# Two heads at once on the array's halves in attention and in the recurrence's chunk products, and modulation matmuls tied in fours

## The chip, the cores and the metric

The kernel runs on one core of a Trainium2 chip. The metric is the device time of one execution in microseconds (us). TensorE (PE in the profile, its weight loads PEld), VectorE (DVE), ScalarE (ACT) and GpSimd (POOL) each work through their own queue of instructions in order and wait for each other by semaphores; SyncE (SP) issues the transfers from memory. Matmul results land in PSUM, from where VectorE and ScalarE take them.

## The reference

Two decoder layers over 256 tokens of width 2048. In each, a vector `c` gives shifts, scales and gates (the modulation), one input projection feeds two groups of 16 heads of 64, and an output projection and a squared-ReLU MLP of width 8192 follow. Group A is RWKV-7 (a recurrence with a matrix state for each head), group B sparse attention with compressed, selected and window branches. At 256 tokens all four blocks of 64 tokens are selected and the window covers everything, so both of the latter are causal attention, each with keys and values of its own.

```
mod = silu(c) @ w_ada[i] + b_ada[i]            # six vectors of 2048: shift, scale, gate, twice
u = (x * (1 + sc_m) + sh_m) @ w_in[i]
# group A, per head:  sa = S @ -kk;  S = S * w + sa (kk a)^T + v k^T;  o = S @ r
# group B, per head:
p_cmp = softmax(where(cmask, q @ kc.T * scale, NEG)) * cmask      # 15 compressed keys
o = g0 * p_cmp @ vc + g1 * softmax(mask(q @ ks.T * scale)) @ vs + g2 * softmax(mask(q @ kw.T * scale)) @ vw
x = layer_norm(ALPHA * x + (1 + gt_m) * (concat(o_A, o_B) @ w_out[i]))
x = layer_norm(ALPHA * x + (1 + gt_f) * (relu(h @ w1)**2 @ w2))
```

## The kernel before

Activations are kept transposed, 128 features on the partitions and the 256 tokens along the row. The projections (`block`, L243, and `kouter`, L256) split each fp32 weight into a high part `wh` and a low part `wl` (`unit`, L218: one DMA of 512 KB, a cast on ScalarE, a subtraction on VectorE) and do three fp32r products for each pair of operands (`mm3`, L235). `block` makes one output tile of 128 rows from 48 matmuls; `kouter` makes eight at once, going through the inputs one by one. All other matmuls are plain fp32, and each of them stands in the trace as two records. The program is written in order of computation; a planner then puts every engine's instructions into a fixed order, by priority (by default the place in the program) and by when it expects operands and buffers to be ready. `tc.high_priority` raises the priority of what is traced inside it, and `tc.issue_after(ins)` makes what is traced inside it come after `ins` on the same engine. Tiles are taken from named groups of buffers: `st(tag, ...)` in SBUF, with the counts of `BUFS` (L175; one where no count stands), and `mx(th, ...)` in PSUM, one bank for `"m"` and `"n"`, two for `"a"` and `"c"`.

The modulation of layer 0 is made on TensorE by `ada_pe` (L357): for a group of 512 outputs, four steps, each of four matmuls. A matmul takes 128 rows of the weight (`wap`, 512 columns, in memory order from the `wad` tensors) as the moving operand and the vector, repeated over 32 columns, as the weights, and writes one quarter of the 128 partitions of `gv` (L369). The first eight groups run in the opening stage (`first`, `start`), whose TensorE order is the program's own. The other twelve (`mid_ada`, L689) are drawn step by step by `spread` and `extra` beside the projections of layer 0: the first seven groups with two DMAs of 512 KB a step (tag `wf`), the last five with four DMAs of 256 KB a step (tag `UR`, eight buffers). Layer 1's modulation and the rest of layer 0's are made on VectorE (`ada`, L334).

The recurrence works in chunks of 64 tokens. `rwkv_a` (L483) prepares a pair of heads (one on partitions 0 to 63, one on 64 to 127); for each head it builds the operand `ur` on VectorE, makes four chunk products `mt` of 64 by 128 by 128 (L530), masks and copies them out, and transposes (`bkt`, L541). There are four pairs in each half and two halves in each layer. `rwkv_b` inverts the chunk's triangular matrices, `rwkv_c` goes through the four chunks, `rwkv_out` normalises.

Attention (`attend`, L823) goes through eight pairs of heads `j`; `q` holds a pair's queries on both partition halves. It makes the compressed scores `cs` and their softmax, transposes them (`ct`), and opens the pair's output `o` (L851). Then for each of two branches `br` and each head `h` in turn: scores `sc` of 128 and 256 columns on the head's half of the rows (L856, L857), masked maxima on VectorE (L861, L862), exponentials with sums on ScalarE (L863, L864), reciprocal, gate and scaling (L865 to L868), three transposes into `pt` (L871), a copy to `pts` (L873), and two products into the head's half of the columns of `o` (L875, L876). The next pair's query projection, and in layer 1 the output projection's `kouter`, can run between.

## Time and profile before

| | us |
|---|---|
| time, median of 3 runs | 2917.93 |
| the runs | 2905.41, 2917.93, 2918.88 |
| the profiled execution, its own time | 2923.44 |
| its span, from the first to the last instruction | 2921.7 |
| PE busy in it | 2804.9 |
| DVE busy | 2103.1 |
| ACT busy | 1507.3 |

Durations below come from the profiled execution. "Busy" counts an engine from an instruction's start to its end; consecutive matmuls overlap in time, so a record's own duration is longer than the distance to the next start. The granted clock of TensorE is given as a share of full speed. An entry such as `gv<-wap,cT 128*32 128x512 f32 x8` reads: written tile, read tiles, the part of the array in use (rows by columns), the moving operand, and how many records follow each other.

### The profile page before, as it was taken

What the parts mean: (1) busy time and instruction counts of PE and PEld (TensorE: products, weight loads), DVE (VectorE), ACT (ScalarE), POOL (GpSimd) and SP (SyncE); (2) the same over time, 40 slices, a digit from 0 to 9 for tenths busy, and PEclk for the clock granted to TensorE, in tenths of its full rate; (3) what the DMA queues carried; (4) which work ended last, traced back from release to release, by engine and by line L of the source; (5) the groups of instructions that cost most, each with busy time, mean ns of one, the idle gap of its engine ahead of it and who ended that gap; (6) DMA issues with size and microseconds to landing.
All of it is one profiled execution on the core that took longest, in us unless ns stands there. A gap on an engine that the chain in (4) does not pass through costs nothing. (4 is left out here: it accounts for less than half of the span.)

```text
span 2921.7 us, 59534 instructions
## 1 busy us (share of the span) xinstructions
PE 2804.9 (96%) x22794; PEld 2502.9 (86%) x22794; DVE 2103.1 (72%) x4774; ACT 1507.3 (52%) x3221; POOL 68.6 (2%) x205
## 2 busy tenths in 40 slices
PE   7989999999999999999999999999999999999997
PEld 4677677745998999999999988887799999999997
DVE  3677768635787777888889787785788656666567
ACT  3344345534474454554645553455657555464555
POOL 0000010000000000000000000100000000000000
PEclk9999999999999999999999998998999999999998
DMA  9986655355658888888887634342275767777663
GB/s 319 315 261 213 238 193 158 103 172 194 221 171 309 308 307 305 319 312 316 320 317 229 191 115 165 107 128 63 80 253 174 243 207 238 234 223 223 194 191 129
DMA packets 206782, 639.64 MB, mean 219 GB/s; under 512 B 23392, under 2 KB 42848, under 8 KB 206496
## 3 DMA queue, kind: packets, MB, share of 16 engines
q1 hardware_dynamic: 206496, 635.83, 65.6%
q8 instruction: 179, 2.93, 0.4%
q14 instruction: 107, 0.88, 0.1%
HBM read 629.45 MB, written 6.29 MB: 218 GB/s over the span
## 5 line engine op out<-in xcount | busy, mean ns | idle before, releaser
L226 ACT CAST wh<-wf 128x512 fp32r<-128x512 f32 x1536 | 944.7, 620 | 916.3 <-PE acc L206 570.5
L227 DVE TENSOR_TENSOR wl<-wf,wh 128x512 fp32r<-128x512 f32 x1536 | 1032.2, 688 | 339.2 <-ACT wh L226 328.8
L206 PE MATMUL acc<-hhi,wl 128*128 128x256 f32 x3456 | 979.5, 284 | 22.0 <-DVE wl L227 21.7
L206 PE MATMUL acc<-hhi,wh 128*128 128x256 f32 x3456 | 982.1, 284 | 15.8 <-ACT wh L226 9.3
L206 PE MATMUL acc<-hlo,wh 128*128 128x256 f32 x3456 | 971.8, 282 | 0.0
L206 PE MATMUL acc<-hi,wl 128*128 128x256 f32 x2560 | 719.9, 281 | 19.5 <-DVE wl L227 19.0
L206 PE MATMUL acc<-lo,wh 128*128 128x256 f32 x2560 | 715.3, 280 | 2.0 <-DVE lo L215 2.0
L206 PE MATMUL acc<-hi,wh 128*128 128x256 f32 x2560 | 714.5, 279 | 1.0 <-DVE res L1030 0.7
L206 PEld LDWEIGHTS acc<-hhi,wh 128*128 128x128 f32 x3456 | 655.3, 190 | 69.8 <-issue 34.6
L206 PEld LDWEIGHTS acc<-hhi,wl 128*128 128x128 f32 x3456 | 655.2, 190 | 48.1 <-DVE wl L227 32.0
L206 PEld LDWEIGHTS acc<-hlo,wh 128*128 128x128 f32 x3456 | 654.1, 189 | 12.8 <-issue 9.2
L206 PEld LDWEIGHTS acc<-hi,wl 128*128 128x128 f32 x2560 | 483.7, 189 | 30.4 <-DVE wl L227 25.9
L206 PEld LDWEIGHTS acc<-lo,wh 128*128 128x128 f32 x2560 | 483.5, 189 | 5.3 <-DVE lo L215 2.6
L206 PEld LDWEIGHTS acc<-hi,wh 128*128 128x128 f32 x2560 | 483.6, 189 | 4.5 <-issue 1.8
L341 DVE CUSTOM_DVE_ANT_0 wa<-wa,cond,modh 128x1024 f32<-128x1024 f32 x112 | 143.6, 1282 | 58.6 <-DMA wa<-in_wada 58.0
L341 DVE CUSTOM_DVE_ANT_0 wa<-wa,cond,vec 128x1024 f32<-128x1024 f32 x112 | 143.6, 1282 | 46.8 <-DMA wa<-in_wada 46.5
L206 PE MATMUL gv<-wap,cT 128*32 128x512 f32 x640 | 149.0, 617 | 8.5 <-DMA wap<-in_wad 7.8
L288 DVE TENSOR_TENSOR sum<-sum,acc 128x512 f32<-128x512 f32 x70 | 48.0, 686 | 47.4 <-PE acc L206 47.4
L1070 DVE TENSOR_TENSOR lo<-relu,hi 128x256 fp32r<-128x256 f32 x128 | 53.9, 424 | 34.9 <-ACT relu L1069 34.8
L206 PE MATMUL sc<-Kd,q 64*128 64x128 f32 (+1 forms) x256 | 64.6, 366 | 0.0
L206 PE MATMUL ot<-pts,Vt 128*64 128x256 f32 (+1 forms) x256 | 57.7, 344 | 0.9 <-DVE pts L873 0.9
L206 PEld LDWEIGHTS gv<-wap,cT 128*32 128x32 f32 x640 | 21.3, 108 | 40.3 <-issue 12.3
(294 smaller groups left out, 2504.0 us busy)
## 6 DMA issues: line engine op xcount, KB each, us to landing
wf<-in_w SPq DMA_DIRECT2D x512, 512.0 KB, 4.8
wa<-in_wada SPq DMA_DIRECT2D x224, 512.0 KB, 5.3
wf<-in_win SPq DMA_DIRECT2D x192, 512.0 KB, 4.1
wap<-in_wad SPq DMA_DIRECT2D x208, 256.0 KB, 4.1
wf<-in_wout SPq DMA_DIRECT2D x64, 512.0 KB, 4.5
wap<-in_wad SPq DMA_DIRECT2D x56, 512.0 KB, 4.6
cw<-in_cw SPq DMA_DIRECT2D x16, 512.0 KB, 3.8
xin<-in_xT SPq DMA_DIRECT2D x16, 128.0 KB, 5.8
```

What stands on the lines that cost most here:

```text
L206: return PE.matmul(o, l, r, start=start, stop=stop, skip_group_check=True)
L226: A.copy(wh, wf[:, s])
L227: V.tensor_sub(wl, wf[:, s], wh.bitcast(FT))
L288: V.tensor_add(s, s, bank)
L341: V.tensor_tensor_reduce(wa, wa, cb, 0.5, init, OP.mult, OP.add, dst)
L1070: gate[0] = V.tensor_sub(lo, t, hi.bitcast(FT)).ins
```

## The change

Three places are rewritten. In `ada_pe` the last of a step's four matmuls is traced first, and the other three are traced with a high priority and an edge that keeps them behind it on TensorE. In `rwkv_a` the operands of both heads are built first, into two banks, and the chunk products alternate between the heads, chunk by chunk; evictions follow, head by head. In `attend` both heads of a pair are handled together within a branch: their scores go to two banks of group `"a"`, the first one carries a dependency on the maximum last traced, and the other three follow it; reciprocals and gates are made for both at once; transposes and copies are grouped by key block instead of by head (`PT0` 512 columns on ScalarE, `PT1` 256 columns on VectorE, one buffer each), and the products into `o` run for both heads one behind the other. The compressed scores move from bank `"n"` to bank `"m"`, the output `o` from the two banks `"a"` to the one bank `"n"`, and `P` holds both heads in one tile for each branch.

```diff
--- before.py
+++ after.py
@@ -173,7 +173,7 @@
         psp = ctx.enter_context(tc.tile_pool(name="psp", bufs=1, space=PSUM))
         drp = ctx.enter_context(tc.tile_pool(name="drp", bufs=1, space=bass.MemoryType.DRAM))
         BUFS = {"S": 52, "OG": 4, "wf": 5, "wh": 4, "wl": 4, "UR": 8, "TM": 8, "BK": 8, "SV": 2, "QB": 2, "ZV": 2, "Us": 2, "rk": 4, "sh": 2,
-                "loa": 1, "loc": 1, "sm": 2, "PT": 2, "pc": 2, "tya": 6, "tyc": 6, "tyn": 8,}
+                "loa": 1, "loc": 1, "sm": 1, "pc": 2, "tya": 6, "tyc": 6, "tyn": 8,}
 
         def st(tag, shape, dt=FT, name=None):
             if dbg is not None:
@@ -364,9 +364,14 @@
                     part = src[u0 + u * n // 2].rearrange("p (a b) -> p a b", a=2)
                     SY.dma_start(w, part if n == 2 else part[:, u % 2:u % 2 + 1])
                     ws += [w[:, k] for k in range(n)]
-                for c in range(4):
+                def part_mm(c):
                     kt = 4 * q + c
-                    mm(gv[c * 32:c * 32 + 32], cT[:, kt:kt + 1].to_broadcast([128, 32]), ws[c], q == 0, q == 3)
+                    return mm(gv[c * 32:c * 32 + 32], cT[:, kt:kt + 1].to_broadcast([128, 32]), ws[c], q == 0, q == 3).ins
+
+
+                with tc.issue_after(part_mm(3)), tc.high_priority(3000000):
+                    for c in range(3):
+                        part_mm(c)
                 yield
             w = 512 // len(gs)
             for i, g in enumerate(gs):
@@ -518,16 +523,19 @@
 
                 V.scalar_tensor_tensor(sq, r, vc(l, "rk", pi), kp, op0=OP.mult, op1=OP.mult)
 
-                for h in range(2):
-                    me, ot = slice(h * 64, h * 64 + 64), slice(64 - h * 64, 128 - h * 64)
+                halves = [(slice(h * 64, h * 64 + 64), slice(64 - h * 64, 128 - h * 64)) for h in range(2)]
+                mts = [mx("a", [128, 4, 128], "mt") for h in range(2)]
+                for h, (me, ot) in enumerate(halves):
                     ur, tm = st("UR", [128, 4, 128]), st("TM", [128, 4, 128])
                     H["UR"][p][h], H["TM"][p][h] = ur, tm
                     G.memset(tm, 0.0)
                     V.tensor_mul(ur[me, :, 0:64], c4(kkn)[me], P[me, :, 0:64])
                     V.tensor_mul(ur[me, :, 64:128], c4(r)[me], P[me, :, 1:65])
-                    mt = mx("a", [128, 4, 128], "mt")
-                    for c in range(4):
-                        mm(mt[:, c], bk[me, c, h:h + 2].rearrange("p a b -> p (a b)"), ur[me, c])
+                for c in range(4):
+                    for h, (me, ot) in enumerate(halves):
+                        mm(mts[h][:, c], bk[me, c, h:h + 2].rearrange("p a b -> p (a b)"), H["UR"][p][h][me, c])
+                for h, (me, ot) in enumerate(halves):
+                    ur, tm, mt = H["UR"][p][h], H["TM"][p][h], mts[h]
                     rm = cs("rmask")
                     V.tensor_mul(ur[ot], mt[ot], rm[ot, None, :].to_broadcast([64, 4, 128]))
                     V.tensor_mul(tm[me, :, 64:128], mt[me, :, 64:128], rm[me, None, 64:128].to_broadcast([64, 4, 64]))
@@ -818,13 +826,13 @@
                 for a in range(2):
                     A.copy(Vt[i][a], va[i][:, a * T:a * T + T])
 
-            last_ins = [None]
+            last_ins, last_max = [None], [None]
 
             def attend(j, q):
                 gp = j // 4
 
                 pc = st("pc", [128, 2, 2, 16])
-                s = mx("n", [128, 2, 2, 16], "cs")
+                s = mx("m", [128, 2, 2, 16], "cs")
                 for i in range(2):
                     mm(s[:, i].rearrange("p a b -> p (a b)"), q[:, i * 128:i * 128 + 128], kcd[:, gp].rearrange("p a b -> p (a b)"))
                 mask = lambda n: cs(n).rearrange("p (a b) -> p a b", a=2)[:, :, None, :].to_broadcast([128, 2, 2, 16])
@@ -847,33 +855,47 @@
                     PE.transpose(ct[:, i * 128:i * 128 + 128], pc[:, i].rearrange("p a b -> p (a b)"), ident)
                 cts = st("a5", [32, T], name="cts")
                 A.copy(cts, ct)
-                o = mx("a", [128, T], "ot")
+                o = mx("n", [128, T], "ot")
                 mm(o, vcb[:, gp], cts, True, False)
+                am = cs("amask")
+                rows = [slice(h * 64, h * 64 + 64) for h in range(2)]
                 for br in range(2):
+
+                    ss = [mx("a", [128, 384], "sc") for _ in range(2)]
+                    score = lambda h, c, n: mm(ss[h][:, c:c + n], q[rows[h], c:c + 128], Kd[br][gp][rows[h], 0:n])
+                    ins = score(0, 0, 128).ins
+                    if last_max[0]:
+
+                        tc.add_manual_dep(ins, last_max[0].name, mybir.DependencyInfo(mybir.DependencyClass.Sync, mybir.DependencyReason.DATA), reason="pair")
+                    with tc.issue_after(ins), tc.high_priority(3000000):
+                        score(1, 0, 128)
+                        score(0, 128, 256)
+                        score(1, 128, 256)
+                    P = st("a9" if br else "sm", [128, 2, 384], name="P")
+                    m, z = tiny("n", 4), tiny("n", 4)
                     for h in range(2):
-                        rows = slice(h * 64, h * 64 + 64)
-                        s = mx("n", [128, 384], "sc")
-                        mm(s[:, 0:128], q[rows, 0:128], Kd[br][gp][rows, 0:128])
-                        mm(s[:, 128:384], q[rows, 128:256], Kd[br][gp][rows])
-                        P = st("a9" if (j * 4 + br * 2 + h) % 3 == 2 else "sm", [128, 384], name="P")
-                        m, z = tiny("n", 2), tiny("n", 2)
-                        am = cs("amask")
-                        V.tensor_tensor_reduce(P[:, 0:128], s[:, 0:128], am[:, 128:256], -0.125, 3e38, OP.add, OP.min, m[:, 0:1])
-                        V.tensor_tensor_reduce(P[:, 128:384], s[:, 128:384], am, -0.125, 3e38, OP.add, OP.min, m[:, 1:2])
-                        A.activation(P[:, 0:128], P[:, 0:128], AF.Exp, bias=m[:, 0:1], scale=-1.0, accum_out=z[:, 0:1])
-                        A.activation(P[:, 128:384], P[:, 128:384], AF.Exp, bias=m[:, 1:2], scale=-1.0, accum_out=z[:, 1:2])
-                        V.reciprocal(z, z)
-                        V.tensor_mul(z, z, gj[:, :, h, 1 + br])
-                        V.tensor_scalar(P[:, 0:128], P[:, 0:128], z[:, 0:1], None, op0=OP.mult)
-                        A.mul(P[:, 128:384], P[:, 128:384], z[:, 1:2])
-                        pt = mx("m", [128, 384], "pt")
-                        for i in range(3):
-                            PE.transpose(pt[:, i * 128:i * 128 + 128], P[:, i * 128:i * 128 + 128], ident)
-                        pts = st("PT", [128, 384], name="pts")
-                        last_ins[0] = (A.copy if h == 0 else V.tensor_copy)(pts, pt).ins
-                        g = gp * 2 + h
-                        mm(o[rows, 0:T], Vt[0][br][:, g * 64:g * 64 + 64], pts[:, 0:256], False, False)
-                        mm(o[rows, 128:T], Vt[1][br][:, g * 64:g * 64 + 64], pts[:, 256:384], False, True)
+                        for i, (c, n) in enumerate(((0, 128), (128, 256))):
+                            last_max[0] = V.tensor_tensor_reduce(P[:, h, c:c + n], ss[h][:, c:c + n], am[:, 256 - n:256], -0.125, 3e38,
+                                                   OP.add, OP.min, m[:, 2 * h + i:2 * h + i + 1]).ins
+                            A.activation(P[:, h, c:c + n], P[:, h, c:c + n], AF.Exp, bias=m[:, 2 * h + i:2 * h + i + 1], scale=-1.0,
+                                         accum_out=z[:, 2 * h + i:2 * h + i + 1])
+                    V.reciprocal(z, z)
+                    zi = z.rearrange("p (h i) -> p i h", h=2)
+                    V.tensor_mul(zi, zi, gj[:, :, :, 1 + br])
+                    for h in range(2):
+                        V.tensor_scalar(P[:, h, 0:128], P[:, h, 0:128], z[:, 2 * h:2 * h + 1], None, op0=OP.mult)
+                        A.mul(P[:, h, 128:384], P[:, h, 128:384], z[:, 2 * h + 1:2 * h + 2])
+                    for i in range(2):
+                        n = 256 - 128 * i
+                        pt = mx("m", [128, 2, n], "pt")
+                        for h in range(2):
+                            for c in range(n // 128):
+                                PE.transpose(pt[:, h, c * 128:c * 128 + 128], P[:, h, 256 * i + c * 128:256 * i + c * 128 + 128], ident)
+                        pts = st(f"PT{i}", [128, 2, n], name="pts")
+                        last_ins[0] = (A.copy if i == 0 else V.tensor_copy)(pts, pt).ins
+                        out = lambda h: mm(o[rows[h], 128 * i:T], Vt[i][br][:, gp * 128 + h * 64:gp * 128 + h * 64 + 64], pts[:, h], False, i == 1)
+                        with tc.issue_after(out(0).ins), tc.high_priority(3000000):
+                            out(1)
                 mix[8 + j] = q
                 A.copy(q, o)
 
```

## Rows read from the trace of the kernel before

**Rows 1.** The page's own head and its first two parts: busy time, share and count of each engine over the span, then the busy share in tenths of 40 slices of 73 us for PE, and the granted clock in tenths.

```profile
PE 2804.9 (96%) x22794; PEld 2502.9 (86%) x22794; DVE 2103.1 (72%) x4774; ACT 1507.3 (52%) x3221; POOL 68.6 (2%) x205
...
PE   7989999999999999999999999999999999999997
PEclk9999999999999999999999998998999999999998
```

**Rows 2.** Busy time of every engine in stretches (columns: the stretch and its length; then for PE, PEld, DVE, ACT and POOL the busy us and, in brackets, the instructions; granted clock, share of the DMA engines, GB/s). 182 to 486 us is the recurrence of layer 0 with its projections, 486 to 711 its attention (it ends with ScalarE's last copy of an attention output), 1630 to 1941 and 1941 to 2108 the same in layer 1.

```profile
182.00:486.00 304.00, 290.36 (x2245) 219.95 (x2243) 227.54 (x621) 139.20 (x343) 23.98 (x82) 0.97 0.62 209
486.00:711.00 225.00, 222.18 (x1437) 129.64 (x1436) 114.24 (x464) 99.86 (x307) 5.65 (x12) 0.98 0.45 143
586.00:711.00 125.00, 124.33 (x525) 52.77 (x523) 45.61 (x208) 44.96 (x137) 0.36 (x2) 1.00 0.53 170
1630.00:1941.00 311.00, 300.48 (x2467) 265.40 (x2466) 247.49 (x648) 158.52 (x366) 19.73 (x67) 0.97 0.44 138
1941.00:2108.00 167.00, 165.11 (x1301) 126.67 (x1301) 114.44 (x461) 96.47 (x299) 5.62 (x10) 0.95 0.23 70
```

**Rows 3.** The same view of the stretches, for the instructions on the modulation tile gv alone (first PE column: busy us and number of matmul records).

```profile
182.00:486.00 304.00, 51.48 (x256) 10.43 (x256) 1.32 (x8) 4.73 (x14) 0.97 0.62 209
586.00:711.00 125.00, 62.34 (x180) 10.25 (x180) 0.87 (x5) 2.92 (x5) 1.00 0.53 170
```

**Rows 4.** The order of time on PE around one undivided modulation step in the start of layer 0 (columns: start, duration from the first start to the last end, engine, line, operation, out<-in, array tile, moving operand, count).

```profile
42.24 0.28 PE L206 MATMUL acc<-hlo,wh 128*128 128x256 f32 x1
42.45 1.07 PE L206 MATMUL gv<-wap,cT 128*32 128x512 f32 x8
43.45 0.38 PE L206 MATMUL acc<-hhi,wh 128*128 128x256 f32 x1
43.67 0.28 PE L206 MATMUL acc<-hhi,wl 128*128 128x256 f32 x1
```

**Rows 5.** The same view in the attention of layer 0, a few us of it.

```profile
605.14 1.04 PE L206 MATMUL gv<-wap,cT 128*32 128x512 f32 x2
606.11 0.39 PE L206 MATMUL acc<-hlo,wh 128*128 128x256 f32 x1
...
608.14 0.66 PE L377 MATMUL gv<-cst,gs 128*128 128x128 f32 x4
```

**Rows 6.** PE in order of time around one head's scores and around one head's weighted sums, each between products of the next projection.

```profile
488.17 0.28 PE L206 MATMUL acc<-hhi,wh 128*128 128x256 f32 x1
488.38 0.92 PE L206 MATMUL sc<-Kd,q 64*128 64x128 f32 x4
489.23 0.39 PE L206 MATMUL acc<-hhi,wl 128*128 128x256 f32 x1
489.45 0.28 PE L206 MATMUL acc<-hlo,wh 128*128 128x256 f32 x1
489.57 0.28 PE L206 MATMUL acc<-hhi,wh 128*128 128x256 f32 x1
...
507.74 0.86 PE L206 MATMUL ot<-pts,Vt 128*64 128x256 f32 x4
```

**Rows 7.** The stretch view again, for the scores (sc) in the two attention stretches, and for the chunk products (mt) in the two recurrence stretches.

```profile
486.00:711.00 225.00, 31.99 (x128) 17.48 (x128) 21.30 (x64) 0.98 0.45 143
1941.00:2108.00 167.00, 32.56 (x128) 17.82 (x128) 21.56 (x64) 0.95 0.23 70
...
182.00:486.00 304.00, 18.72 (x128) 15.50 (x128) 17.68 (x32) 15.96 (x48) 0.97 0.62 209
1630.00:1941.00 311.00, 18.29 (x128) 15.44 (x128) 17.74 (x32) 16.13 (x48) 0.97 0.44 138
```

**Rows 8.** PE in order of time: chunk products of one head; then sixteen small products on alternating column halves; then four on the whole array with a moving operand of two columns.

```profile
222.64 1.13 PE L206 MATMUL mt<-UR,a 64*128 64x128 f32 x8
...
350.08 0.69 PE L206 MATMUL up<-SV,UR 128*64 128x64 f32 x16
...
233.40 0.60 PE L206 MATMUL tp<-cst,a 128*128 128x2 f32 x4
```

**Rows 9.** VectorE in order of time: the last operand that the first head's chunk products wait for, and the second head's.

```profile
222.08 0.41 DVE L515 SCALAR_TENSOR_TENSOR a<-a,a 128x256 f32<-128x256 f32 x1
222.87 0.42 DVE L527 TENSOR_TENSOR UR<-rk,a 64x256 f32<-64x256 f32 x1
```

**Rows 10.** The view of one tile, wap: the DMA issues of the modulation weights (duration of one issue in ns, min/median/max); what PE stood idle for (us, times); the time from issue to landing.

```profile
L365 SPq DMA_DIRECT2D wap<-in_wad x264: 327/373/1540, 2.6 to 694.9; - x132
  DMA wap<-in_wad: 18.6, 22
DMA to landing us min/median/max: 2.4/4.4/7.1
```

**Rows 11.** Groups of VectorE and ScalarE by line in the attention (busy us, mean ns of one, idle time before, releaser).

```profile
L862 DVE CUSTOM_DVE_ANT_0 P<-sc,cst 128x256 f32<-128x256 f32 x64 | 26.6, 415 | 0.0
...
L868 ACT ACTIVATE P<-P,tyn 128x256 f32<-128x256 f32 x64 | 32.4, 507 | 13.6 <-DVE tyn L866 10.6 <-DVE tyn L840 2.6
L864 ACT ACTIVATE P<-P,tyn 128x256 f32<-128x256 f32 x64 | 31.9, 498 | 0.6 <-DVE tyn L862 0.4
L873 ACT COPY pts<-pt 128x384 f32<-128x384 f32 x32 | 15.2, 476 | 17.9 <-PE pt L871 17.8
```

## The prediction

> **What bounds the kernel now.** I read the page's head first: PE is busy for 2805 of 2921.7 us, no other engine for over 72%, and the slices show PE at nine tenths nearly everywhere at full clock [rows 1]. A busy PE need not be working hard, so I next asked each stretch whether PE waits. In the four stretches that the edit touches PE is busy for 290 of 304, 222 of 225, 300 of 311 and 165 of 167 us, with VectorE at 75, 51, 80 and 69% [rows 2]. There PE's own instruction stream is the bound, and what leaves it leaves the span, as long as other work is ready behind it. So the question is the price of each kind of work on PE, read in order of time.
>
> The reader is to see three prices. The ordinary stream of projection products starts one about every 0.115 us (489.45, 489.57) [rows 6]. A detour costs more than its own duration: around one head's scores the start of the last product before to the second one after is 489.45 - 488.17 = 1.28 us; less two ordinary steps (0.23) that is 1.05 us for 384 moving columns, which take 0.64 us (0.86 us for four records of the same columns in the weighted sums, less a tail of about 0.22) [rows 6]. So some 0.4 us of every detour is entry and exit. And a modulation step is four matmuls of two records each on four column quarters of the array: all eight together take 1.07 us [rows 4], and two of the eight alone take 1.04 [rows 5]. The quarters run side by side; a step that is broken up pays the full price for every piece.
>
> **Modulation steps.** From 182 to 486 us there are 28 steps (256 records less 8 groups of four transposes are 224, by eight). Their PE time is 51.5 us; less 8 x 0.66 for the transposes [rows 5] it is 46.2, and by 1.05 that is 44 passes where 28 would do [rows 3]. Among projection products a pass costs 43.67 - 42.24 - 0.23 = 1.20 us [rows 4], so the 16 passes too many cost 19 us. From 586 to 711 us there are 20 steps (160 records) in 62.3 - 5 x 0.66 = 59.0 us: 56 passes, 36 too many [rows 3]. Their neighbours are mostly other detours, so I price them at 1.05 us: 38 us. A control stands in the trace: the same attention without modulation work takes 167 us in layer 1 and 225 us in layer 0 [rows 2]; the 58 us between them are the 56 passes at about one us. Tying removes the pieces because the last quarter to land is issued first and the other three follow without a gap. In the start of layer 0 the steps are whole already [rows 4], and I take nothing there.
>
> **Scores.** Each pair of heads now issues four matmuls alternating between the row halves, into two banks. No row of before shows two row halves at work together, so this is bounded from both sides. If they overlap as the column parts do, 16 pairs a layer at one head's 0.92 us replace 32 us of PE time [rows 6, 7]: a gain of 17 us a layer. If the halves take turns, a pair costs 1.28 + 0.28 = 1.56 us, in one detour in place of two: 32 - 25 = 7 us. Between them lies a shared path for weights: 128 columns of weights take (0.60 - 0.28)/3 = 0.11 us each even when only two columns move (0.28 is one record's own duration) [rows 6, 8], eight of them 0.88 us, a pair then about 1.16 us and the gain 13. I take 17: the nearest row is the pair of column halves, whose sixteen records of 64 columns end in 0.69 us, against 16 x 0.053 + 0.22 = 1.07 in turn [rows 8].
>
> **Weighted sums.** These go onto column halves, first 256 columns for both heads, then 128. One head costs 0.86 us [rows 6]; a pair now costs (0.43 + 0.22) + (0.21 + 0.22) = 1.08 where two heads cost 1.72. 16 pairs a layer: 10 us. The transposes are as many as before, in fewer pieces: 1 to 2 us. Attention thus frees about 29 us of PE time a layer. The Trainium skill speaks against this part: its page TensorE: Matmul & The Clock Gate, section Part 3, says a weight load overlaps running matmuls only when the row groups differ, and column halves share theirs; by that rule the weighted sums would gain nothing, which is the sixth rival. The trace differs: the column halves in [rows 8] end in two thirds of the time that turns would take.
>
> **Chunk products.** A head's eight records take 1.13 us [rows 8], 18.7 and 18.3 us in the two recurrences [rows 7]. Paired fully, 16 pairs replace 32 singles: 9 us a layer. But the first head's operands are complete at 222.5 and the second's at 223.3 us [rows 9], so PE may run through most of the first head before it can alternate, and at 128 moving columns the weight path (0.11 us each) is as long as the moving itself. Bounds 0 and 9 a layer; I take 5, a merged detour and a little overlap.
>
> **On VectorE and ScalarE** a pair of heads saves one reciprocal and one multiply, and its copies stay. All four maxima, then the exponentials, then one reciprocal: behind that reciprocal VectorE's later work stands until the last exponential has ended. A branch has two large maxima at 0.42 us and two small ones, two large exponentials at 0.50 and two small ones beside them, two scales at 0.51 and copies of which one of 384 columns takes 0.48 [rows 11]; I estimate some 4 us from the first maximum to the last scale, in which the next branch's scores, other products and the branch before can run on PE. I cost it at nothing while PE has that other work; without it, it is the third rival. The new dependency of a pair's first score on the last maximum delays nothing that the second head's bank did not delay anyway. Scores get two banks in place of one; the outputs one in place of two; the small compressed scores and all transposes share one bank, a copy after each.
>
> **What comes next in each place.** In the first recurrence 14 of 304 us are PE idle, and VectorE is at 75% [rows 2]: I pass on three quarters of 19 + 5, that is 18 us. In layer 0's attention PE would lose 38 + 29 = 67 us, but the modulation weights arrive through eight buffers, now freed in fours: four issues of 0.37 us, 4.4 us to landing, 1.2 us of PE, with two steps in flight, make (1.5 + 4.4 + 1.2)/2 = 3.5 us a step [rows 4, 10], 71 us for 20 steps from 586, so not before 657 where it now ends at 711. I take 50 us. In layer 1's second recurrence 4 of 5, and in its attention, where the output projection can start on finished heads and fills PE, 26 of 29. The other stages issue the same work. The sum is 18 + 50 + 4 + 26 = 98 us. The profiled execution took 2923.4 us (span 2921.7), which gives 2825; it stands 5.5 us above the median of the runs, 2917.9, against which I put the forecast: **2820 us**, with bounds of its own from 2798 (19 + 9 + 54 + 9 + 29 = 120 us: everything but the buffer floor) to 2845 (18 + 35 + 2 + 18 = 73 us: little overlap on the row halves, two thirds of layer 0's attention).
>
> **The rivals.**
> 1. The array's row halves take turns. The scores give 7 and not 17 a layer, the chunk products 3. Layer 0's attention is still near its buffer floor (48), so the sum is 17 + 48 + 3 + 18 = 86: 2832 us. For it: no row shows the overlap. Against: column parts overlap in every row that has them. Chance 0.14.
> 2. Everything that leaves PE leaves the span: the buffer floor does not bind because steps slip behind the next stage's first products, and chunk products pair. 19 + 9 + 67 + 9 + 29 = 133: 2785 us. Chance 0.12.
> 3. Attention becomes a chain. One bank for compressed scores and transposes, one for the outputs: if nothing overlaps, a turn is two branches of 0.92 + 4 + 1 (transposes) + 1 (copies), plus 3 for the compressed softmax, about 17 us. Layer 1 then keeps its 167 us, layer 0 gains perhaps 40 from the modulation steps: 17 + 40 + 3 = 60, 2858 us. Against: both score banks are free again after the maxima. Chance 0.13.
> 4. Slower: PE's queue is in order, and a tied step stands at its head for the piece that lands last. Wherever the planned order is ahead of the real transfers, PE stands still with everything behind it. From a mean wait of 98/48 = 2.0 us in each of the 48 steps of the middle stages this eats the gain; at the full 4.4 us to landing [rows 10] it costs 211 us against 98, 3031 us. Against: PE stood idle for these transfers for 18.6 us in the whole span, 22 times [rows 10]. Chance 0.05; a milder form, 1.8 to 2.2 us a step, comes out within 0.5%.
> 5. The planned order does not place the partners side by side, other instructions stand between, and nearly all stays: 2905 to 2925 us. Chance 0.04.
> 6. Column halves take turns after all: the weighted sums gain nothing, 98 - 18 = 80, 2838 us. Against: the sixteen records in 0.69 us [rows 8]. Chance 0.02.
>
> **How the numbers follow.** The forecast has 0.50. Rivals 1 to 3 and 6 are faster too, which makes 0.91; I keep 0.04 of the third and the mild fourth for "same" and "slower", because the whole order of instructions is planned anew with such an edit: faster by over 0.5% 0.87, within 0.5% (about what a measurement of this kernel can tell from no change) 0.06, slower 0.07. The range takes in rivals 1 to 3 and 6 with some 10 us around them: 2772 to 2872.
>
> **What would show it.** Right: gv passes near 48 in the middle stages, each x8 at 1.07 us; score detours x8 in 0.9 to 1.0 us for two heads; layer 0's attention taking near 175 us in place of 225, layer 1's near 140 in place of 167. Rival 1: x8 scores at 1.5 us. Rival 3: PE idle growing in the attention, for VectorE's scales and ScalarE's copies. Rival 4: PE waits named by wap. Wrong altogether would be an unchanged number of pieces, or stages after the attention that grow by what it lost.

## The result, and the profile after

The changed kernel takes 2850.7 us (median of four runs, 2848.3 to 2857.4) against 2918.4 for the kernel before on the same chip: a ratio of 0.978 [0.975, 0.980]. On another chip it took 2841.8 against 2914.3, 0.975 [0.973, 0.977]. The forecast was 2820, so of 98 us some 68 to 73 came. The profiled execution has a span of 2848.2 us, 73.5 below that of before.

The page's head after, with its slices of PE and of the granted clock, answers to [rows 1]:

```profile
PE 2699.9 (95%) x22794; PEld 2460.7 (86%) x22794; DVE 2088.5 (73%) x4710; ACT 1507.6 (53%) x3221; POOL 69.3 (2%) x205
...
PE   7999899998999999999999999999999999999997
PEclk8999999999999999999999999999999999999998
```

PE issues the same 22794 records and is busy 105 us less, yet the span fell by only 73.5: PE's idle time rose by 31 us. The stretches after say where. The first six answer to [rows 2] (both recurrences, both attentions, and layer 0's attention cut where the modulation steps end); the last two are an attention together with its output projection, up to the norm's scale.

```profile
182.00:476.00 294.00, 276.69 (x2256) 219.18 (x2254) 229.07 (x626) 138.69 (x344) 24.47 (x82) 0.97 0.63 217
476.00:655.00 179.00, 162.49 (x1465) 111.04 (x1465) 107.53 (x436) 101.59 (x311) 5.91 (x12) 0.95 0.56 182
564.00:636.00 72.00, 65.48 (x493) 34.65 (x485) 36.12 (x172) 40.22 (x124) 0.00 (x0) 1.00 0.84 273
636.00:655.00 19.00, 13.40 (x77) 7.50 (x73) 9.49 (x45) 9.64 (x30) 0.36 (x2) 0.74 0.30 110
1563.00:1877.00 314.00, 303.13 (x2473) 266.51 (x2471) 247.87 (x647) 159.67 (x369) 20.13 (x68) 0.98 0.43 136
1877.00:2048.00 171.00, 160.14 (x1474) 127.35 (x1474) 118.81 (x447) 105.22 (x316) 5.23 (x10) 0.96 0.30 95
...
476.00:752.00 276.00, 251.25 (x2196) 197.48 (x2197) 182.13 (x590) 148.14 (x401) 5.91 (x12) 0.96 0.61 199
1877.00:2121.00 244.00, 227.06 (x2008) 192.79 (x2009) 181.42 (x587) 139.35 (x380) 5.23 (x10) 0.96 0.42 138
```

The same two stretches of the kernel before:

```profile
487.00:813.00 326.00, 316.03 (x2192) 220.29 (x2192) 190.85 (x624) 147.72 (x401) 5.65 (x12) 0.97 0.52 168
1941.00:2195.00 254.00, 249.63 (x2005) 209.66 (x2005) 187.37 (x617) 140.16 (x379) 5.62 (x10) 0.97 0.41 131
```

Read the last rows in pairs. In layer 0 PE's work falls by 65 us and its idle time grows from 10 to 25: 50 come out. In layer 1 the work falls by 23 and the idle time grows from 4 to 17: 10 come out. These two stretches hold 27 of the 31 us.

The stretch view by tile, modulation (gv) first, then scores (sc), then chunk products (mt), answers to [rows 3, 7]:

```profile
182.00:476.00 294.00, 35.10 (x256) 8.14 (x256) 1.34 (x8) 4.65 (x14) 0.97 0.63 217
476.00:655.00 179.00, 24.51 (x180) 5.26 (x180) 0.87 (x5) 2.93 (x5) 0.95 0.56 182
...
476.00:655.00 179.00, 14.82 (x128) 8.38 (x128) 21.31 (x64) 0.95 0.56 182
...
182.00:476.00 294.00, 16.05 (x128) 13.56 (x128) 17.17 (x32) 16.25 (x48) 0.97 0.63 217
1563.00:1877.00 314.00, 17.90 (x128) 15.20 (x128) 17.58 (x32) 16.29 (x48) 0.98 0.43 136
```

Modulation work fell from 51 to 35 and from 62 to 25 us, the scores from 32 to 15; the chunk products hardly moved. In order of time on PE, an undivided step, a pair's scores and its two weighted sums, which answer to [rows 4 to 6]:

```profile
600.12 1.06 PE L206 MATMUL gv<-wap,cT 128*32 128x512 f32 x8 [0.49 <-DMA wap<-in_wad]
...
2021.10 0.93 PE L206 MATMUL sc<-Kd,q 64*128 64x128 f32 x8
...
2029.66 0.65 PE L206 MATMUL ot<-pts,Vt 128*64 128x256 f32 x4
...
2031.20 0.44 PE L206 MATMUL ot<-pts,Vt 128*64 128x128 f32 x4
```

Eight score records of two heads take 0.93 us, as four of one head took before. What PE waited for in layer 0's attention and output projection, then in layer 1's (us, times, longest):

```profile
PE gv L206 <- DMA wap<-in_wad: 5.8, 6, 1.6
PE acc L206 <- DVE res L1052: 2.6, 1, 2.6
...
PE ot L206 <- ACT pts L895: 1.5, 3, 0.7
PE pt L893 <- DVE P L886: 1.3, 2, 1.0
...
PE acc L206 <- DVE res L1052: 4.0, 2, 2.8
PE ot L206 <- ACT pts L895: 1.9, 4, 0.7
```

There is no single large wait: modulation weights, the copies and scales of the attention, and VectorE's work behind the norm's mean each take a few us.

ScalarE's copies of the attention outputs show the turns; the last two of layer 0 and of layer 1:

```profile
638.09 0.37 ACT L900 COPY q<-ot 128x256 f32<-128x256 f32 x1 [1.24 <-PE ot L206]
654.36 0.37 ACT L900 COPY q<-ot 128x256 f32<-128x256 f32 x1 [3.05 <-PE ot L206]
...
2031.71 0.37 ACT L900 COPY q<-ot 128x256 f32<-128x256 f32 x1
2047.50 0.37 ACT L900 COPY q<-ot 128x256 f32<-128x256 f32 x1 [3.05 <-PE ot L206]
```

15 to 17 us a pair (the last four turns of either layer; the first three of layer 1 take 20 to 27). The last two copies of layer 1 before:

```profile
2095.82 0.37 ACT L878 COPY q<-ot 128x256 f32<-128x256 f32 x1 [1.84 <-PE ot L206]
2107.61 0.37 ACT L878 COPY q<-ot 128x256 f32<-128x256 f32 x1 [0.63 <-PE ot L206]
```

The last three turns of layer 1 took 12 to 13 us there. The pairs cost PE less, and these end further apart.

### The profile page after: what moved, and what is told of

The parts are those of the page before. It is cut to its first block, busy times and chain, and to the rows that moved or that the text cites. A ratio compares the mean times of both kernels' runs of the same rounds, so it can differ in the third digit from the quotient of the medians.

```text
span 2848.2 us, 59407 instructions
## 1 busy us (share of the span) xinstructions
PE 2699.9 (95%) x22794; PEld 2460.7 (86%) x22794; DVE 2088.5 (73%) x4710; ACT 1507.6 (53%) x3221; POOL 69.3 (2%) x205
## 4 chain that ended last, share of the span: by engine, by line
PE 60%; DVE 15%; DMA 15%; issue 5%; ACT 4%; SPq 0%; ACTq 0%; DVEq 0%; POOL 0%
PE acc L206 47%; DMA wa<-in_wada 11%; DVE wl L227 6%; PE gv L206 2%; DVE wa L341 2%; ACT wh L226 2%; DMA wap<-in_wad 1%; PE ot L206 1%; DMA wf<-in_w 1%; PE mt L206 1%; PE pt L893 1%; DMA wf<-in_win 1%; PE va L206 1%; DVE Tt L574 1%; DVE fs L572 1%
## 5 line engine op out<-in xcount | busy, mean ns | idle before, releaser
L206 PE MATMUL gv<-wap,cT 128*32 128x512 f32 x640 | 89.3, 631 | 23.8 <-DMA wap<-in_wad 21.4
L880 ACT ACTIVATE P<-P,tyn 128x128 f32<-128x128 f32 (+1 forms) x128 | 57.2, 448 | 11.2 <-DVE tyn L878 10.1
L1090 ACT ACTIVATE hi<-relu 128x256 fp32r<-128x256 f32 x128 | 53.5, 422 | 3.5
L1091 ACT ACTIVATE relu<-relu 128x256 f32<-128x256 f32 x128 | 53.3, 420 | 3.6
```

The costliest lines, as they stand in the source:

```text
L206: return PE.matmul(o, l, r, start=start, stop=stop, skip_group_check=True)
L880: A.activation(P[:, h, c:c + n], P[:, h, c:c + n], AF.Exp, bias=m[:, 2 * h + i:2 * h + i + 1], scale=-1.0, accum_out=z[:, 2 * h + i:2 * h ...
L1090: A.activation(hi, t, AF.Square)
L1091: A.activation(t, t, AF.Square)
```

## Experiments

**One part at a time.** Three kernels, each with one part of the diff.

e1_ties, only the modulation steps:

```
+    with tc.issue_after(part_mm(3)), tc.high_priority(3000000):
+        for c in range(3):
+            part_mm(c)
```

> Of the change only the tied modulation steps are kept; attention and chunk products are those of before. My theory (a broken-up step pays the full price of a pass for every piece, and PE has other work behind it): passes fall from 128 to 80 or less, PE busy by 54 us, layer 0's recurrence by 11 us, its attention by about 40, the total by about 50 us, to 2868 (ratio 0.983). Rival (the weights' eight buffers hold the steps back, and the gain of the whole change came from attention): PE waits for wap in place of the passes, a gain under 20 us.

Measured: 0.984 [0.981, 0.987], 49 us below its before. Layer 0's attention with the output projection:

```profile
478.00:762.00 284.00, 272.88 (x2193) 212.36 (x2192) 191.15 (x622) 147.77 (x401) 5.76 (x12) 0.98 0.60 192
```

PE's work falls by 43 us from before's 316 and the stretch by 42: here a saving passes on whole.

e2_attn, only `attend` and its buffers (the part of the diff from `last_max` on):

> Of the change only attention by pairs of heads is kept; modulation steps and chunk products are those of before. My theory (a pair of heads is now a chain of 15 to 16 us through the one bank that holds compressed scores and transposes): layer 0's attention, which took 22 to 25 us a pair because PE was full of modulation passes, falls by 25 us; layer 1's keeps its length and only the output projection's products move into its idle time, 10 to 15 us: together about 40, 2878 us (0.986). Rival (no chain; the loss in layer 1 came from the other edits): 50 to 58 us, 2865.

Measured: 0.988 [0.985, 0.991], 38 us. Layer 0's and layer 1's attention with output projection:

```profile
491.00:796.00 305.00, 287.16 (x2197) 208.03 (x2198) 184.59 (x592) 149.51 (x401) 6.00 (x12) 0.95 0.56 180
1922.00:2159.00 237.00, 222.83 (x2001) 189.89 (x2000) 180.31 (x584) 139.15 (x379) 5.29 (x10) 0.97 0.44 140
```

PE's work falls by 29 and 27 us, close to the 29 of the forecast; 21 and 17 reach the length.

e3_chunks, only the alternating chunk products:

> Of the change only the alternating chunk products are kept. My theory (the planned order runs the first head's four products before the second's operands are ready, so that hardly any pair overlaps): mt busy stays at 33 to 37 us, the total within 5 us of before, 2918 (0.999). Rival (they overlap and something else hides it): mt busy near 18 us.

Measured: 1.002 [1.000, 1.004], `mt` busy for 14.4 and 17.9 us in the two recurrences. Alone this part gains nothing. The three give 49, 38 and -4, together 83; the whole change gave 68 to 73. The missing dozen is not clear of the intervals of the three (5 to 9 us each). The profiles, one execution each, put it in layer 0: 42 and 21 are 63, and both together brought 50 there (53 in a second profile of the changed kernel, after_again below).

**The attention's chain.** e4_cmp_ahead traces the compressed branch of the next pair before the present pair's two branches, so that its softmax is done before the pair's own turn:

```
-            def attend(j, q):
+            def compressed(j, q):
...
+                return pc
+
+            def attend(j, q, pc):
...
+                    qs.append((q, compressed(j, q)))
+                if j == 0:
+                    continue
+                j -= 1
+                attend(j, *qs[j])
```

> The changed kernel with one reordering: the compressed scores and their softmax of the next pair of heads are traced before the branches of the present pair, in the same bank. My theory (the chain through that bank ends a pair with the last copy and starts the next with scores, softmax, transposition, some 5 of 15 to 16 us): a pair takes 11 to 12 us in layer 1, PE idle in both attentions falls, layer 0 gains up to 15 us (its modulation steps need 72 us through their buffers) and layer 1 about 8: 2828 us (0.969). Rival (the turn of a pair is set by VectorE and ScalarE inside the branches): within 4 us of the changed kernel, 2850.

Measured: 2853.2 us, 0.979 [0.975, 0.982]: no gain, and the time that the rival forecast. The head of the list of what PE waited for in layer 1's attention and output projection, to set against that of after:

```profile
PE acc L206 <- DVE res L1063: 4.8, 2, 2.6
PE hp L206 <- DVE O L585: 1.9, 1, 1.9
```

The waits of the weighted sums (`ot`) have left the head of the list, and others have grown. The two stretches are 271 and 242 us, 5 and 2 shorter than after. That does not show in the time: the first recurrence is 3 us longer, and layer 0's feed-forward stretch, which the edit doesn't touch, took 718 us in this profile and 712 in both profiles of the changed kernel. What that stretch follows (707 to 718 us over all profiles, before 717) was not settled.

ScalarE's last two copies of layer 1 in e4, and VectorE's wait for the last pair's compressed scores, which e4 makes in the turn of the pair before:

```profile
2041.44 0.37 ACT L905 COPY q<-ot 128x256 f32<-128x256 f32 x1
2051.12 0.37 ACT L905 COPY q<-ot 128x256 f32<-128x256 f32 x1
...
2026.53 0.23 DVE L839 TENSOR_TENSOR pc<-cs,cst 128x64 f32<-128x64 f32 x1 [1.39 <-PE cs L206]
```

The three turns before the last take 14.8 to 15.5 us, as after, and not the 11 to 12 of my theory. The last one takes 9.7 (after: 15.8), and it is the only one beside which no further pair's compressed branch runs. In the others that branch still stands at the head of the turn: VectorE waits there for `cs` as it did after (1.1 to 1.4 us), and the present pair's maxima come behind it. So the reordering moved the softmax to another pair's turn and did not take it out. That the pairs would be faster without it is neither shown nor refuted by this run; that moving it gains time is refuted.

**Chunk products tied.** e5_tied_chunks issues them as one block in turns, the second head's first:

```
+    with tc.issue_after(chunk(1, 0)), tc.high_priority(3000000):
+        chunk(0, 0)
+        for c in range(1, 4):
+            chunk(1, c)
+            chunk(0, c)
```

> The changed kernel with the chunk products tied like the modulation steps: the second head's first product is issued first, the other seven follow without a gap. If row halves overlap at 128 columns as they do in the scores, 16 groups of sixteen records take 1.1 to 1.2 us each, mt busy falls from 34 to 18 us, and the two recurrences together by 10 to 12 us: 2840 us (0.973). Rival (at 128 columns the loading of weights is as long as the product and is shared): 1.9 us a group, and the total within 4 us of the changed kernel. Second rival (waiting for both heads delays the inverse behind them): the groups are short and the total is the same.

Measured: 0.978 [0.976, 0.979], no gain over the change. In order of time on PE, then the two recurrences, then PE's longest wait in the first:

```profile
433.95 1.16 PE L206 MATMUL mt<-UR,a 64*128 64x128 f32 x16 [0.19 <-DVE UR L533]
...
202.00:480.00 278.00, 258.86 (x2131) 200.96 (x2129) 210.34 (x585) 127.37 (x322) 22.55 (x73) 0.95 0.64 217
1564.00:1880.00 316.00, 298.51 (x2490) 262.74 (x2488) 247.59 (x642) 160.75 (x373) 19.99 (x70) 0.97 0.43 138
...
PE bkt L555 <- ACT TM L552: 5.5, 9, 1.2
```

The products themselves do what pairing can do: sixteen records in 1.16 us, where eight took 1.13 [rows 8]. PE's work in the second recurrence is 298.5 us in place of 305.0, and the recurrence is as long. The transposes `bkt` behind the products now wait for ScalarE 5.5 us (after: 1.1). This is the outcome of the second rival. That the recurrence's own chain through both heads takes the time that PE gave up is my reading of that wait; in the first recurrence the granted clock was also lower, 0.95 for 0.97, and PE's work there stayed at 259 us although `mt` fell from 16 to 9.3.

e6_both is e4 and e5 together:

> The changed kernel with both mendings, compressed scores one pair ahead and tied chunk products. If they are independent, as one acts in the attentions and the other in the recurrences: the sum of their gains, about 2818 us (0.966). If the earlier chunk products only bring the attention's chain forward into the same wait: no better than the better one of the two.

Measured: 0.981 [0.979, 0.982]; nothing adds.

**The ring of weight buffers.** e7_quarter_loads leaves out three of four loads of the modulation weights in the attention:

```
+                ws = ws if once and q else []
+                for u in range(4 * q // n, 4 * (q + 1) // n) if not ws else ():
```

> The changed kernel, but the 20 modulation passes that run in layer 0's attention use the weights of the first quarter four times: 15 of 20 quarters' loads (four buffers each) are left out, so the modulation values computed there are others; TensorE's, VectorE's and ScalarE's instructions are the same. It asks whether the ring of weight buffers still sets the end of that attention. Theory (it does not: the passes end at 635.5 of 654.7 us, and the last pairs are a chain): the passes end earlier, the attention's length stays within 5 us of 178.8 us, the time within 5 us of the changed kernel's 2850.7. Rival (the ring, as the prediction had it): the 5.8 us in which TensorE waits ahead of these passes and what their loads take from the other weights come out, the attention takes 165 to 170 us, and the time is 2838 to 2842.

Measured: 2853.3 us, 0.979 [0.977, 0.981]; that is 11 us above the changed kernel on the same chip, 6 of them in the recurrence ahead, which is not the question here. Layer 0's attention, its part with modulation steps, and what is left; then the attention in after_again, the changed kernel on that chip:

```profile
480.00:655.00 175.00, 164.53 (x1463) 113.39 (x1462) 107.61 (x434) 101.42 (x310) 5.91 (x12) 0.92 0.30 96
570.00:618.00 48.00, 47.28 (x368) 23.39 (x360) 24.94 (x121) 26.44 (x83) 0.00 (x0) 1.00 0.31 102
618.00:655.00 37.00, 31.16 (x202) 19.83 (x198) 21.23 (x95) 22.98 (x71) 0.36 (x2) 0.81 0.09 29
...
473.00:649.00 176.00, 161.23 (x1465) 109.02 (x1465) 107.23 (x436) 100.99 (x310) 5.90 (x12) 0.96 0.56 186
```

The steps end after 48 us in place of 71, so the ring did pace them. The attention is as long as the changed kernel's on the same chip (176), and the last pairs stand alone for 37 us in place of 20 (from 629 on there), so the ring doesn't set the end. The last four turns take 14 to 17 us here and 15 to 18 in after_again; that the pairs' chain sets the end is what is left, read from these turns. One reservation: over the whole attention the granted clock is 0.92 here and 0.96 in after_again, that is 14 and 7 us of full speed lost (an estimate, share times length). A gain of some 7 us by the ring could hide in that.

**VectorE behind the norm's mean.** e8_norm_gpsimd moves that work to GpSimd; e9_ahead_norm_gpsimd adds e4; after_again is the changed kernel beside them.

```
-                        V.tensor_sub(x, x, N["m0"])
+                        G.tensor_sub(x, x, N["m0"])
...
-                    V.tensor_add(N["sq"], N["sq"], x)
+                    G.tensor_add(N["sq"], N["sq"], x)
```

> The changed kernel with the subtraction of the first estimate of the mean from eight tiles and the sums of squares of the layer norms on GpSimd instead of VectorE. It asks whether VectorE's burst behind the mean is what is late next in the output projections: TensorE waits 2.6 us (layer 0) and 2.8 and 1.1 us (layer 1) there for an eviction, where the kernel before waited 0.5 and 0.2. Theory: these waits go, 4 to 6 us, 2845 to 2847 us; and the output projection after layer 1's attention shortens by about 3 us. Rival: GpSimd's 0.74 us for one such operation against VectorE's 0.42 makes the sums late at the norms' ends, where TensorE waits for them with nothing else to do: no gain, or a loss of up to 10 us over the four norms (2851 to 2861).

> The run before and the compressed branch of the next pair traced ahead of the present pair (as in e4_cmp_ahead) together. Theory: waits in the attention's chain and in the output projections both go; e4 cut the stretch from layer 0's first compressed score to its norm by 4.7 us and layer 1's by 1.4, so 2840 to 2844 if they add. Rival: PE's waits move on to something else again, 2848 to 2856.

> The changed kernel as it is, on the same chip as the three above, so that differences of a few us can be told: 2848 to 2857 as before. If the layer 0 feed-forward stretch (711.5 us in the profile after, 715 to 718 in most other profiles) is again near 711, that stretch's gain belongs to the change; if it is 715 or more, it was one execution's.

Measured: 2877.7 (0.987 [0.986, 0.989]), 2884.1 (0.989 [0.987, 0.992]) and 2841.8 us (0.975 [0.973, 0.977]). The rival's direction, over three times as large (36 us against its 10). Its mechanism accounts for 26 of the 36: the four norms, each from the mean to the scale, are 5.8, 8.1, 5.9 and 6.2 us longer than in the profile after; the rest was not followed. From the mean to the norm's scale layer 0 now takes 55 us where the changed kernel takes 49, GpSimd is busy for 18 us with 22 operations, and PE stands idle for 5.6 us in place of 1.7:

```profile
704.00:759.00 55.00, 49.44 (x401) 47.20 (x402) 36.17 (x69) 26.06 (x51) 18.00 (x22) 1.00 0.56 174
```

Whether the waits for evictions cost anything by themselves stays open; this was the wrong tool to take them away. No version beat the change.

**Less work in the attention.** e10_less_work_after and e11_less_work_before leave out a third of the query projections' matmuls:

```
-            mm(o, wl, xh, False, False)
-            mm(o, wh, xl, False, last)
+            mm(o, wl, xh, False, two and last)
+            if not two:
+                mm(o, wh, xl, False, last)
```

> The changed kernel, with one of the three products of each query projection in the attention (the low part of the input by the high part of the weight) left out: 16 matmuls for each of 8 pairs and 2 layers, 256 matmuls that follow each other every 0.113 us in full rows, 28.9 us of TensorE's work that is not in the attention's own chain and has no work of another engine tied to it. It asks how much of a TensorE saving still reaches the time after the change. Theory (in the changed kernel the chain from scores to copies and the waits behind it share the end with TensorE): a third to three quarters of it comes out, 10 to 21 us below the changed kernel on one chip (2841.8 there, so 2821 to 2832; a ratio of 0.968 to 0.972). Rival (TensorE is still the bound everywhere): 27 us or more, 2815 or below.

> The kernel before with the same 256 matmuls left out. Both theories: TensorE is idle for 2 us in each of these attentions, so nearly all of the 28.9 us comes out, 25 to 29 us, a ratio of 0.990 to 0.9915. If less than 20 us come out, a saving in these stretches was never worth its full size and the prediction's sum was wrong there for the kernel before as well.

Measured: 2868.4 us, 0.984 [0.982, 0.986], and 2927.6 us, 1.004 [1.003, 1.005]. Both are slower with 29 us less to do, which neither theory had (the changed kernel's ratios are 0.975 and 0.978). The two attentions with their output projections, of e10 and then of e11:

```profile
469.00:761.00 292.00, 256.41 (x2079) 193.50 (x2078) 183.85 (x595) 149.52 (x400) 5.65 (x12) 0.89 0.59 188
1884.00:2139.00 255.00, 228.37 (x1888) 188.46 (x1889) 180.74 (x587) 140.07 (x378) 5.04 (x10) 0.88 0.40 131
```

```profile
483.00:810.00 327.00, 315.75 (x2076) 214.82 (x2076) 191.11 (x628) 149.43 (x400) 5.88 (x12) 0.93 0.52 168
1928.00:2196.00 268.00, 250.76 (x1890) 204.48 (x1891) 188.63 (x622) 139.57 (x378) 5.65 (x10) 0.91 0.39 125
```

Two things moved. The order was planned anew: in layer 0 of the kernel before, PE issues 123 projection products between the first pair's compressed scores and the second's, and 208 more up to the last pair's; in e11 it is 222 and 52, and in e10 229 and 45 where the changed kernel has 164 and 219. The products run early, and the later pairs have few beside them. And PE is granted 0.88 to 0.93 of its clock where it had 0.96 and 0.97, so that the remaining products fill as much busy time as before. In the two stages of e10 PE is busy for 485 us against 478 after and idle for 62 against 42; in e11 busy for 567 against 566 before and idle for 28 against 14. By share times length (an estimate) the clock costs e10 63 us of full speed there, and the changed kernel 21. Why the clock fell isn't shown, and no run varies the order and the clock apart. So these runs don't measure what a saving is worth, as they were meant to. They show that a plan with less filler can lose more than the 29 us that were left out.

## Why the prediction was right and wrong

Its direction and its range held, and so did its prices on PE but that of the chunk products. By stage (first recurrence, first attention, second recurrence, second attention, the rest) the forecast was 18 + 50 + 4 + 26 + 0 = 98 us, and between the two profiled spans, which differ by 73.5 us, they gave 11, 50, -2, 10 and about 4. The main steps:

- **Modulation steps.** 48 passes of 1.06 us, as forecast. The ties alone gave 49 us, two thirds of the change.
- **Scores.** 0.93 us for two heads (forecast 0.92): the row halves overlap in full, and the first rival falls. The Trainium skill, page TensorE: Matmul & The Clock Gate, section Part 3, lets weight loads overlap matmuls on other row groups; this row agrees.
- **Weighted sums.** 0.65 and 0.44 us (forecast 0.65 and 0.43); the sixth rival falls. That the section's rule on weight loads leaves column halves no gain was the prediction's own inference; the same section's table lists a gain for column tiles, and these rows agree with the table.
- **Chunk products.** Forecast 5 us of PE a layer; they measured 2.7 and 0.4. Most heads' products ran before their partner's operands were there. In e5 the full pairing did not help: the recurrences keep their length. The first recurrence gave 11 us for 18 (from its first group projection on, 202.5 to 486.7 before and 202.8 to 475.9 after); there PE's work fell by 14 and its idle time took back 3.
- **Layer 0's attention.** Forecast 50, measured 46, with the output projection 50. The size was right and the reason wrong: the steps did end after 72 us (forecast 71), but the attention went on for 19 more, and in e7 it ended no earlier without the ring, at a lower granted clock.
- **Layer 1's attention**, forecast 26, measured 10 with the output projection. This is the step that failed: "I cost it at nothing while PE has that other work". PE's work fell by 23 us, and 13 of it came back as idle time. The attention itself took 171 us for 167, where 140 was to be the sign of a right prediction; the gain came in the output projection behind it, 73 us for 87. The third rival named the mechanism and this outcome for layer 1, with turns of 17 us; the last four are 15 to 16. Which link of the chain holds a turn stays open, as e4 left the compressed branch in it. Not all of the shortfall is the chain's: in e2, with the same instructions in another order, this stage gave 17. PE was about as idle in the attention (10 us, after 11), and the granted clock was 1.00 in place of 0.96:

```profile
1921.60:2086.40 164.80, 154.85 (x1473) 123.48 (x1473) 117.99 (x445) 105.03 (x314) 5.29 (x10) 1.00 0.32 97
```

- **Other stages.** Forecast nothing; they gave 4.9 us around layer 0's feed-forward network and took 2.4 in layer 1's recurrence. The first came in both profiles of the changed kernel; its cause is open.

The fourth rival's waits grew and stayed far below the 98 us that would have eaten the gain. What PE stood idle for modulation weights in the whole span (us, times, longest), after and before:

```profile
PE gv L206 <- DMA wap<-in_wad: 21.4, 10, 9.6
...
PE gv L206 <- DMA wap<-in_wad: 7.8, 4, 7.0
```

The prediction's 18.6 us [rows 10] are these 7.8 and 10.8 of PEld, so they are not all PE's. Of the 13.6 us more, 5.8 lie in layer 0's attention, where there were none, and the others in the opening stage, which ends where it did before (202.8 and 202.5 us). So tying the steps to the piece that lands last did cost PE waits, but few where the change saves its time.

## What to carry to other kernels

Price an instruction on TensorE by its detour, then ask stage by stage how much other work is left beside the chain once it is shorter: passes without a chain behind them gave their full price here (43 us of work, 42 of time), those inside a softmax chain from under half to three quarters. Two savings in one stage need not add up (63 us alone, 50 together); that they draw on the same filler is a reading that no run tests. Before shortening work further, look at where the plan puts the filler and at the granted clock: here, with less filler, both kernels became slower.

## What was not expected of the hardware

Records on the two row halves run side by side even for 128 moving columns and 128 columns of weights each: sixteen in 1.16 us where eight took 1.13, and eight scores in 0.93 where four took 0.92. And the granted clock can take back a saving: in e10 and e11 the same stages ran at 0.88 to 0.93 with less work, where they had 0.96 and 0.97. What sets it isn't settled by PE's busy share alone. In e7 it is 1.00 over 48 us in which PE is busy for 47.3, and 0.81, an average of time at 2.4 and at 1.2 GHz, over the 37 us after, in which it is busy for 31.2. But the kernel before has a stretch in layer 1's attention with PE busy nearly throughout, at 0.79:

```profile
1980.80:2020.80 40.00, 39.73 (x486) 29.96 (x483) 20.09 (x82) 19.64 (x73) 5.31 (x9) 0.79 0.18 54
```
